# Turning two more block pairs on VectorE, all of them loaded by SyncE, with later stores and smaller warm-up matmuls, in a matmul with rotary embedding

## The chip, the cores and the metric

The kernel runs on one NeuronCore of one Trainium2 chip. The metric is device time in microseconds (us), the median of the runs shown; a change is given as a difference from it.

## The reference

```python
batch, seq, hidden, n_heads = (16, 512, 768, 12)
...
y = np.matmul(x, weight)                       # (16, 512, 768) x (768, 768)
y = y.reshape(batch, seq, n_heads, head_dim)   # head_dim 64
y1, y2 = y[..., :32], y[..., 32:]
out1 = y1 * cos1 - y2 * sin1                   # cos, sin: (seq, 64), one row for each position
out2 = y2 * cos2 + y1 * sin2
out = np.concatenate([out1, out2], axis=-1)    # float32, shape of x
```

All inputs and the output are float32. x and the output have 25.17 MB each.

## The kernel before, in words

**Tiles and groups.** The 8192 rows of x are worked in 64 tiles of 128 rows (`NTILE`), four tiles to a group (`QB`), sixteen groups (`NG`, the last is `LAST` = 15). A tile holds every fourth position of one batch entry (`where`). Two neighbouring tiles of a group are a pair: pair (g, 0) holds tiles 4g and 4g+1, pair (g, 1) the other two.

**From x to the matmul.** TensorE needs x with the hidden dimension on the partitions, in fp16. There are two ways to it, and the dictionary `BLOCKS` says which pair goes which way.

- An ordinary tile is loaded by one DMA of SyncE (SP) into one of `NX` buffers xs (`load`), cast to fp16 by ScalarE (ACT; `castx`, xc), turned by twelve small TensorE (PE) matmuls against an identity (`turn_rows`, L275), and copied from PSUM to an xt buffer by ACT.
- A block pair is loaded in four quarters (`load_quarter`, L229) whose rows are laid out such that VectorE (DVE) alone can finish the turn with one 32x32 block transpose (`turn_pair`, L303). A pair marked "sp" is loaded by SP in float32 into one of `NB` buffers xb, and ACT casts it to xd (`cast_pair`). A pair marked "pool" is loaded by GpSimd's (POOL's) queue, which casts in the DMA, into one of `NBH` buffers xh; ACT has nothing to do for it. PE does nothing for a block pair.

Before the change there are fourteen block pairs, twelve "sp" and two "pool", (4, 1) and (6, 1).

**Order of SP's loads.** The list `fetch` is written ahead. A pair that stands in `EARLY` has its quarters in its tiles' place in the list; the quarters of the others, here (5, 1), (7, 1) and (15, 1), are spread behind ordinary tiles from one to two groups ahead. `pump` takes from the list as far as buffers are free, and the semaphores hold SP until ACT has read the buffer's old content.

**Matmul.** Each tile's 768 columns are made in six steps of the hidden dimension (`CHUNKS`). PE runs two streams, one for each half of its rows, over six PSUM banks that hold one group's 3072 columns (`walk`, `both`, L365). The first group and the last tiles go by L340. The turning of tiles is written into PE's order three tiles ahead (`T_AHEAD`), ACT's casts five (`C_AHEAD`), DVE's block transposes four (`B_AHEAD`).

**Rotary part.** A group is cut into units of 512 or 1024 columns (`units`). For each, DVE multiplies PSUM by cos and sin in one instruction (`rope`, L446) into one of three homes of 3072 numbers, two in tq and one in the weights' raw buffer; POOL adds the products into an output buffer ov (L468). There are four ov buffers, one for each group in turn, so group g writes where group g-4 stood, and its adds wait for the stores of that group.

**Stores.** Groups 0 to 12 are stored in quarters by ACT's queue (`store_half`): quarter n of this sequence (four for each group) is issued at the end of tile i, with i from a formula (L678), after a wait for PE to have come so far. Groups 13 and 14 are stored by SP in halves, and group 15 by SP and ACT in pieces.

**Start.** While the first loads come, PE multiplies zeros (`warm`, L582): nine matmuls ahead of the first tile's turn and three behind it. Each has 128 weight columns and 512 moving columns, and matmul k writes bank k mod 6. The last six also leave the banks at zero for the first group, which adds onto them.

Of the kernel before, what the change touches and what calls it, by code (L numbers as in the profile page):

```python
# [16 lines left out]
class Flow:  # L17
# [24 lines left out]
    def do(self, e, make, reads=(), writes=(), dma=None, tick=True, after=0):  # L42
        need = {}
        for k in reads:
            for s, v in self.wrote.get(k, {}).items():
                need[s] = max(need.get(s, 0), v)
        for k in writes:
            for d in (self.wrote, self.readby):
                for s, v in d.get(k, {}).items():
                    need[s] = max(need.get(s, 0), v)  # L50
        if e == "pe":
            need.pop("pe", None)
            if after:
                need["pe"] = after
        waits = self.settle(e, need)
        for s, v in waits[:-1]:
            self.eng[e].wait_ge(self.sem(s), v)  # L57
        i = make(self.eng[e])
        if waits:
            s, v = waits[-1]  # L60
            i.wait_op(self.sem(s), v, "sem-ge")
        name, step = (dma, 16) if dma else (e, 1)
        self.sem(name)
        self.order[name] = len(self.order) + sum(self.count.values())
        at = self.count[name] + step
        if tick or dma:
            i.then_inc(self.sems[name], step)
            self.count[name] = at
            self.known[name, at] = dict(self.seen[e])
        for k in reads:  # L70
            d = self.readby.setdefault(k, {})
            d[name] = max(d.get(name, 0), at)
        for k in writes:
            self.wrote[k] = {name: at}
            self.readby[k] = {}
        return i
# [32 lines left out]
def kernel(  # L109
# [11 lines left out]
    f = Flow(nc, tc)  # L121
    do = f.do
    P = nc.NUM_PARTITIONS
# [9 lines left out]
    QB = 4  # L133
# [3 lines left out]
    LAST = NG - 1  # L137


    BLOCKS = {}  # L140
    for g in range(5, 14):
        BLOCKS[g, 1] = "pool" if g % 2 == 0 and g >= 4 else "sp"
    BLOCKS[LAST, 1] = "sp"
    BLOCKS[4, 1] = "pool"
    EARLY = ((3, 1), (8, 0), (8, 1), (9, 1), (10, 0), (10, 1), (11, 1), (12, 1), (13, 1))
    for p in EARLY:
        BLOCKS[p] = "sp"

    def sbuf(name, shape, dt):
        return nc.alloc_sbuf_tensor(name, shape, dt).ap()  # L150

    NX, NB, NBH, NC, NCP, NXT, NXP, NOV = 10, 3, 3, 5, 2, 8, 4, 4

    ident = sbuf("ident", [P, P], FP16)
    cold = sbuf("cold", [P, 512], FP16)
# [26 lines left out]
    py = nc.alloc_psum_tensor("py", [P, 6 * 512], FP32).ap()  # L182
# [14 lines left out]
    def where(i):  # L197
        g, s = divmod(i, QB)
        return QB * (g // SB) + s, g % SB

    def pair_of(i):
        return i // QB, (i % QB) // 2

    def is_block(i):
        return pair_of(i) in BLOCKS

# [11 lines left out]
    def load_quarter(gh, q):  # L218
        g, h = gh
        b, r = where(g * QB + 2 * h)  # L220
        e = BLOCKS[gh]
        src = x[b : b + 2].rearrange("b (j a r) (q k) -> r q a (b j) k", r=SB, a=R, q=NQ)
# [282 lines left out]
    def store_half(g, h, c, at):  # L505
# [20 lines left out]
       reads=["ident"], writes=["ident32"])  # L526
# [13 lines left out]
    fetch, quarters = [], []  # L540
    soon = [p for p in sorted(BLOCKS) if BLOCKS[p] == "sp" and p not in EARLY]
    for i in range(QB, NTILE):
# [3 lines left out]
        if not is_block(i):  # L546
            fetch.append(i)
            for _ in range(2 if i == QB * (LAST - 1) else 1):
                if quarters:
                    fetch.append(quarters.pop(0))  # L550
        elif pair_of(i) in EARLY:
            fetch += [(pair_of(i), q) for q in ((0, 2), (1, 3))[i % 2]]
# [23 lines left out]
    WARM = 12  # L576
    warmed = [0]

    def warm(k):
        for _ in range(k):  # L580
            b = warmed[0] % 6
            do("pe", lambda eng: eng.matmul(  # L582
                py[:, ts(b, 512)], cold[:, 0:P], cold, start=True, stop=warmed[0] < WARM - 6),
                reads=["cold"], writes=[f"ps{b}"], tick=False)
            warmed[0] += 1

    def mm0(i, c):
# [10 lines left out]

    U0 = units(0)
    warm(9)  # L600
    castx(0, "act")
    turn(0, "dve")
    castx(1, "act")
    warm(3)
    turn(1, "dve")
    castx(2, "act")
# [13 lines left out]
    for c in CHUNKS[3:5]:  # L620
# [8 lines left out]
        reads=["sin", "csn1", "cos"], writes=["csn"])  # L629
# [45 lines left out]
    stores, halves = {}, {}  # L675
    for n in range(4 * (LAST - 2)):
        g, (h, c) = n // 4, divmod(n % 4, 2)
        i = 5 + n + min(3, n // 5) if g < LAST - 4 else QB * (LAST - 2) + (n - 4 * (LAST - 4)) // 2  # L678
        halves.setdefault(i, []).append((g, 2 * h, c))
    for g in range(LAST - 2, LAST):  # L680
        for h in (0, 2):
# [22 lines left out]
    for i in range(QB, NTILE):  # L704
        g, s = divmod(i, QB)
# [16 lines left out]
        for n, p in enumerate(pieces(g, s)) if i >= ROWS else ():  # L722
# [3 lines left out]
            for c in CHUNKS:  # L726
                mm_piece(i, p, c, c == CHUNKS[0], c == CHUNKS[-1],
                         tick=c == CHUNKS[-1])
# [60 lines left out]
```

## Time and profile before

| what | value |
|---|---|
| median of 3 runs (lowest, highest) | 150.32 us (149.86, 150.71) |
| the profiled execution: its own time, its span | 148.68 us, 146.9 us |
| busy: PE, DVE, POOL, ACT | 140.0, 128.0, 116.7, 76.5 us |
| one turn of a tile: twelve L275 matmuls | 190 ns each in the record, overlapped; 11.6 us busy for 360 |
| ACT: cast of a tile, copy of a turned tile, cast of a pair | 910, 801, 1632 ns |
| DVE: block transpose from xd, from xh | 966 ns x12, 1246 ns x2 |
| DVE: product of 512, of 1024 columns | 1213 to 1220, 2266 to 2268 ns |
| POOL: add of 512, of 1536 columns; issue of one cast load | 1274, 3468 ns; 601 ns x8 |
| DMA | 52.44 MB, mean 357 GB/s |

The profiled execution took 1.8 us more than its span, and 1.64 us less than the median of the runs. PE is busy nearly all the time, but so are DVE and the DMA engines over most of the span; which of them sets the end has to be read stage by stage. The granted clock is shown as 1.00 throughout.

### The profile page before, as it was taken

Reading aid. Unit: us, or ns where it says so; the run is one execution under the profiler, and the core shown is the slowest. Engines: PE = TensorE matmul, PEld = TensorE weight load, DVE = VectorE, ACT = ScalarE, POOL = GpSimd, SP = SyncE. Lnnn points to the kernel's source line nnn. Section 1 sums busy time; section 2 is a strip of 40 time slices with the busy share of each in tenths; the row PEclk is TensorE's granted clock in tenths of the full one; section 3 lists DMA queues with packets and bytes.
Section 4 is the critical chain, followed back from the end, with each engine's and each line's share of the span. In section 5 each row is a group of like instructions: output and inputs, shape, how many; then the busy total and the mean of one; then the engine's idle time right before and its main releaser. Section 6 shows DMA issues by size and latency. Waiting matters only on the chain.

```text
span 146.9 us, 4261 instructions
## 1 busy us (share of the span) xinstructions
PE 140.0 (95%) x1846; PEld 112.1 (76%) x1846; DVE 128.0 (87%) x105; ACT 76.5 (52%) x84; POOL 116.7 (79%) x64
## 2 busy tenths in 40 slices
PE   6969999999999999999999999999999999999980
PEld 2445578888888888888888888888888888765860
DVE  0155999878989999899999999999989899999990
ACT  3453798788242933557442942284664649931010
POOL 2000399999996988959788988989899999899980
PEclk9999999999999999999999999999999999999999
DMA  4999999999999999999999999999999999999684
GB/s 118 379 403 404 402 401 270 263 332 327 329 332 330 339 390 389 383 345 375 377 386 384 389 395 387 396 392 393 385 388 398 392 404 401 394 412 360 267 314 158
DMA packets 37826, 52.44 MB, mean 357 GB/s; under 512 B 4656, under 2 KB 31024, under 8 KB 37808
## 3 DMA queue, kind: packets, MB, share of 16 engines
q1 hardware_dynamic: 21200, 30.42, 59.2%
q10 hardware_dynamic: 14432, 20.97, 38.6%
q0 software_dynamic: 2176, 0.79, 4.3%
q8 instruction: 14, 0.23, 0.6%
q14 instruction: 4, 0.03, 0.1%
HBM read 27.79 MB, written 25.17 MB: 361 GB/s over the span
## 4 chain that ended last, share of the span: by engine, by line
PE 83%; DVE 12%; issue 2%; DVEq 0%; SPq 0%
PE py L365 69%; DVE tq L446 8%; PE py L340 5%; PE py L582 4%; PE pt L275 3%; DVE w_raw L446 2%; PE pt L260 2%; DVE ov L415 1%; DVE py L408 0%; DVE xs L408 0%; DVE xt L194 0%; DVE w_sb L194 0%; DVE cold L519 0%; DVEq L57 0%; DVEq L784 0%
## 5 line engine op out<-in xcount | busy, mean ns | idle before, releaser
L468 POOL TENSOR_TENSOR ov<-tq 128x512 f32<-128x512 f32 (+3 forms) x34 | 76.1, 2258 | 22.4 <-DVE tq L446 21.8
L446 DVE TENSOR_TENSOR tq<-py,csn 128x1024 f32<-128x1024 f32 (+2 forms) x51 | 74.2, 1491 | 2.9 <-PE py L365 1.9
L365 PE MATMUL py<-w_sb,xt 64*128 64x512 f16 (+1 forms) x672 | 64.1, 323 | 0.0
L365 PE MATMUL py<-w_sb,xp 64*128 64x256 f16 (+1 forms) x624 | 58.7, 323 | 0.0
L365 PEld LDWEIGHTS py<-w_sb,xt 64*128 64x128 f16 x672 | 47.3, 94 | 8.8 <-DVE tq L446 0.4
L365 PEld LDWEIGHTS py<-w_sb,xp 64*128 64x128 f16 x624 | 44.2, 94 | 7.2
L194 ACT COPY xt<-pt 128x768 f16<-128x768 f16 x34 | 27.1, 801 | 33.2 <-PE pt L275 31.3
L194 ACT CAST xc<-xs 128x768 f16<-128x768 f32 x36 | 32.5, 910 | 18.3 <-PE py L365 10.5
L468 POOL TENSOR_TENSOR ov<-w_raw 128x1536 f32<-128x1536 f32 (+2 forms) x15 | 35.4, 2372 | 3.0 <-DVE w_raw L446 2.9
L446 DVE TENSOR_TENSOR w_raw<-py,csn 128x1024 f32<-128x1024 f32 (+1 forms) x22 | 35.2, 1600 | 2.5 <-PE py L365 2.1
L194 ACT CAST xd<-xb 128x1536 f16<-128x1536 f32 x12 | 19.6, 1632 | 4.0 <-PE py L365 4.0
L340 PE MATMUL py<-w_sb,xt 128*128 128x256 f16 (+1 forms) x102 | 16.8, 317 | 1.1 <-DVE w_sb L194 1.1
L340 PEld LDWEIGHTS py<-w_sb,xt 128*128 128x128 f16 x102 | 9.4, 98 | 6.7 <-DVE w_sb L194 2.0
L275 PEld LDWEIGHTS pt<-ident,xc 64*128 64x128 f16 x360 | 11.6, 95 | 1.2 <-issue 0.2
L275 PE MATMUL pt<-ident,xc 64*128 64x64 f16 x360 | 11.6, 190 | 0.0
L303 DVE STREAM_TRANSPOSE xp<-xd 128x768 f32<-128x768 f32 x12 | 11.6, 966 | 0.0
L582 PE MATMUL py<-cold 128*128 128x512 f16 x12 | 5.5, 630 | 1.4 <-DVE cold L519 1.4
L194 DVE COPY xt<-pt 128x768 f16<-128x768 f16 x2 | 1.1, 558 | 5.8 <-PE pt L260 5.8
L194 DVE CAST w_sb<-w_raw 128x768 f16<-128x768 f32 x6 | 3.3, 557 | 2.7 <-DMA w_raw<-in_weight_dram 2.6
L194 ACT COPY ov<-py 128x256 f32<-128x256 f32 x1 | 0.4, 372 | 10.0 <-PE py L478 10.0
L229 POOL DMA_DIRECT2D xh<-in_x_dram x8 | 4.8, 601 | 0.0
L582 PEld LDWEIGHTS py<-cold 128*128 128x128 f16 x12 | 1.6, 145 | 3.6 <-issue 2.2
(26 smaller groups left out, 24.5 us busy)
## 6 DMA issues: line engine op xcount, KB each, us to landing
out_dram<-ov ACTq DMA_DIRECT2D x53, 384.0 KB, 7.6
xs<-in_x_dram SPq DMA_DIRECT2D x36, 384.0 KB, 11.7
xb<-in_x_dram SPq DMA_DIRECT2D x48, 192.0 KB, 10.5
out_dram<-ov SPq DMA_DIRECT2D x4, 768.0 KB, 6.0
w_raw<-in_weight_dram SPq DMA_DIRECT2D x6, 384.0 KB, 7.0
xh<-in_x_dram POOLq DMA_DIRECT2D x8, 96.0 KB, 15.3
out_dram<-ov SPq DMA_DIRECT2D x1, 384.0 KB, 2.3
out_dram<-ov SPq DMA_DIRECT2D x3, 128.0 KB, 2.1
```

The costliest lines, as they stand in the source:

```text
L194: eng.copy(out=o, in_=i_) if e == "act" else eng.tensor_copy(out=o, in_=i_)
L229: do(e, lambda eng: eng.dma_start(out=dst[ts(q, R)], in_=src[r, q]), writes=[f"{name}q{q}"], dma=name)
L260: do("pe", lambda eng: eng.transpose(pt[:, t, h, :], src[:, t, h, :], ident), reads=[f"xc{c}", "ident"], writes=[f"pt{k}"], tick=(t, h) == ...
L275: do("pe", lambda eng: eng.transpose(pts[r][:, t, h, :], src[rows, t, h, :], ident[rows, rows]), reads=[f"xc{c}", "ident"], writes=[f"pt{r ...
L303: do("dve", lambda eng: eng.transpose(out=dst, in_=src), reads=rd, writes=[f"xp{z}"])
L340: do("pe", lambda eng: eng.matmul(ps, get(t, h), w_sb[:, t, h, a - s * H : z - s * H], start=start, stop=stop), reads=[key, f"w{t}{h}"], w ...
L365: do("pe", lambda eng: eng.matmul(py[:, a:z], get(t, h)[rows], w_sb[rows, t, h, a - s * H : z - s * H], start=start, stop=not opens and en ...
L415: do("dve", lambda eng: eng.tensor_tensor(out=ov_b[o][:, ds(c0, w)].rearrange("p (h t d) -> p h t d", t=2, d=HD), in0=q.rearrange("p (h t ...
L446: do("dve", lambda eng: eng.tensor_tensor(out=tq.rearrange("p j (h d) -> p j h d", d=D), in0=ps.rearrange("p (h d) -> p h d", d=D) .unsque ...
L468: do(adder, lambda eng: eng.tensor_tensor(out=ov_b[o][:, ds(c0, w)].rearrange("p (h t d) -> p h t d", t=2, d=HD), in0=tq[:, 0].rearrange(" ...
L582: do("pe", lambda eng: eng.matmul(py[:, ts(b, 512)], cold[:, 0:P], cold, start=True, stop=warmed[0] < WARM - 6), reads=["cold"], writes=[f ...
```

## The change

Four things are edited.

1. The block pairs become sixteen, all "sp". New are (6, 0) and (12, 0), so four more tiles are turned by DVE and not by PE; (4, 1) and (6, 1) go from POOL's queue to SP's, and ACT casts them. All pairs but (15, 1) stand in `EARLY`, so that (5, 1) and (7, 1) too have their quarters in their tiles' place. POOL issues no loads.
2. The buffers: eleven xs for ten, four xb for three, no xh for three. The memory is the same.
3. The stores on ACT's queue: quarters 25 to 33 are issued one tile later, 34 to 42 two, and 43 to 51 three (by the formula these are groups 6 to 12).
4. The first six of the twelve matmuls of zeros become eight each, with 64 weight columns and 64 moving columns: 48 in the place of six. They are still ahead of the first tile's turn, and the number of moving columns is the same.

```diff
-    BLOCKS = {}
-    for g in range(5, 14):
-        BLOCKS[g, 1] = "pool" if g % 2 == 0 and g >= 4 else "sp"
-    BLOCKS[LAST, 1] = "sp"
-    BLOCKS[4, 1] = "pool"
-    EARLY = ((3, 1), (8, 0), (8, 1), (9, 1), (10, 0), (10, 1), (11, 1), (12, 1), (13, 1))
+    BLOCKS = {(LAST, 1): "sp"}
+    EARLY = ((3, 1), (4, 1), (5, 1), (6, 0), (6, 1), (7, 1), (8, 0), (8, 1), (9, 1), (10, 0), (10, 1), (11, 1), (12, 0), (12, 1), (13, 1))
     for p in EARLY:
         BLOCKS[p] = "sp"
...
-    NX, NB, NBH, NC, NCP, NXT, NXP, NOV = 10, 3, 3, 5, 2, 8, 4, 4
+    NX, NB, NBH, NC, NCP, NXT, NXP, NOV = 11, 4, 0, 5, 2, 8, 4, 4
...
             b = warmed[0] % 6
-            do("pe", lambda eng: eng.matmul(
-                py[:, ts(b, 512)], cold[:, 0:P], cold, start=True, stop=warmed[0] < WARM - 6),
-                reads=["cold"], writes=[f"ps{b}"], tick=False)
+            n = 64 if warmed[0] < WARM - 6 else 512
+            for c in range(0, 512, n):
+                do("pe", lambda eng: eng.matmul(
+                    py[0:min(P, n), ds(b * 512 + c, n)], cold[:, 0:min(P, n)], cold[:, ds(c, n)],
+                    start=True, stop=warmed[0] < WARM - 6),
+                    reads=["cold"], writes=[f"ps{b}"], tick=False)
...
-        i = 5 + n + min(3, n // 5) if g < LAST - 4 else QB * (LAST - 2) + (n - 4 * (LAST - 4)) // 2
+        i = 5 + n + min(3, n // 5) + max(0, (n - 16) // 9) if g < LAST - 4 else QB * (LAST - 2) + 3 + (n - 4 * (LAST - 4)) // 2
```

## The prediction

> **What bounds the kernel now.** I read the page first: busy shares, slices, DMA.
>
> ```profile
> PE 140.0 (95%) x1846; PEld 112.1 (76%) x1846; DVE 128.0 (87%) x105; ACT 76.5 (52%) x84; POOL 116.7 (79%) x64
> ...
> DMA  4999999999999999999999999999999999999684
> GB/s 118 379 403 404 402 401 270 263 332 327 329 332 330 339 390 389 383 345 375 377 386 384 389 395 387 396 392 393 385 388 398 392 404 401 394 412 360 267 314 158
> ...
> q0 software_dynamic: 2176, 0.79, 4.3%
> ```
>
> PE, DVE and DMA all look full, so shares decide nothing. The chain of waits, in order of time (start, duration), does:
>
> ```profile
> 55.73 0.17 PE pt L275 x10
> 55.91 1.92 PE py L365 x19
> 57.83 0.20 PE pt L275 x11
> 58.03 5.85 PE py L365 x54
> ...
> 124.55 3.44 DVE tq L446 x3
> ...
> 142.91 0.42 DVE ov L415
> ```
>
> From 8.8 to 124.5 us it is PE with no gap: a group with one block pair takes 0.17 + 1.92 + 0.20 + 5.85 = 8.14 us. From 124.55 it is DVE to the end. The timeline of DVE shows how closely it follows (start, duration, in brackets the idle time before):
>
> ```profile
> 59.25 1.23 DVE L446 TENSOR_TENSOR w_raw<-py,csn 128x1024 f32<-128x1024 f32 x1 [0.54 <-PE py L365]
> ...
> 67.40 1.23 DVE L446 TENSOR_TENSOR tq<-py,csn 128x1024 f32<-128x1024 f32 x1 [0.27 <-POOL ov L468]
> ...
> 107.45 1.23 DVE L446 TENSOR_TENSOR w_raw<-py,csn 128x1024 f32<-128x1024 f32 x1 [0.46 <-PE py L365]
> ...
> 115.60 2.36 DVE L446 TENSOR_TENSOR tq<-py,csn 128x1024 f32<-128x1024 f32 x2 [0.53 <-PE py L365]
> ```
>
> These are the third units (second half) of groups 5, 6, 11 and 12. Between 67.4 and 107 us DVE lists no wait, and after 115.60 none before the end stage. So DVE has under 1 us of slack late in the kernel, and a gain on PE only counts if DVE can follow.
>
> **Turning on DVE.** PE loses four tiles' turns (tiles 24, 25, 48, 49). Two cost 0.17 + 0.20 = 0.37 us in the chain, so PE is 0.37 us earlier from tile 26 on and 0.74 from tile 50 on. DVE gains two block transposes. From start to next start one costs 0.89 us (68.54 to 69.43), one from xh 1.17 (60.39 to 61.56); two of the latter become the former. DVE: 2 x 0.89 - 2 x 0.28 = +1.22 us. The ledger, at the third unit of each group:
>
> - group 5: PE delivers at 59.25 - 0.37 = 58.88; DVE was free at 59.25 - 0.54 = 58.71 and has 0.89 more, 59.60. Late by 0.35 against before.
> - group 6: DVE was free at 67.13; + 0.35 - 0.28 = 67.20; PE 67.03. Now 0.20 early.
> - groups 7 to 10: DVE is dense in both kernels; 0.20 early stays.
> - group 11: DVE was free at 106.99; - 0.20 + 0.89 = 107.68, where PE would deliver at 107.45 - 0.74 = 106.71. Late by 0.23.
> - group 12: DVE was free at 115.07; + 0.23 = 115.30; PE 114.86. Early by 0.30.
> - behind it DVE is dense to the end: -0.3 us.
>
> Bounds: -0.74 if DVE overlapped its transposes with waits that the listing doesn't show, +1.22 if none of its idle time could be used. The listed waits (0.54, 0.46, 0.53) are where the ledger uses them, so I take -0.3; reading starts in place of ends (records overlap by up to 0.1) it is -0.5. I use -0.4. PE does not stall on DVE: the largest lag, 107.68 - 106.71 = 0.97 us, compares with 124.55 - (115.60 + 8.15) = 0.80 in group 13 before, which PE rode out.
>
> ACT: four pair casts more (6.5 us), four casts and four copies fewer (4 x 1.711 = 6.8): nothing, at 52% busy. POOL: eight issues fewer, 4.8 us at 24 to 33 us, where it lagged; it waits for DVE afterwards anyway: nothing.
>
> **Loads.** POOL's two pairs held 16 engines for 4.3% of 146.9 = 6.3 us. As 768-byte packets on SP's queue (36 ns each in the packet records) they take 2048 x 36 / 16 = 4.6 us. Two pairs from whole rows (512 packets of 3072 bytes at 122 ns, 3.9 us) to quarters (4.6) cost 0.7. Besides, all traffic ran at 322 GB/s in 26.25 to 50.70 us, with these loads in flight, against 390 in 75 to 99: 24.45 x 68 / 390 = 4.3 us of transfer time. So 3 to 5 us of DMA work go. [...] In the profiled execution the relief is worth nothing on the path: after the start one load alone was late,
>
> ```profile
> ACT xc L194 <- DMA xs<-in_x_dram: 1.5, 1, 1.5
> ```
>
> (waits of 100 to 147 us), five tiles ahead of use, and PE did not notice. SP's queue takes eight more quarters at some 0.5 us, under 9 us of issue in 120. A pair needs four free xb; the fifth before it is cast at least eight tiles (16 us) ahead: covered. If that cover were gone, PE would stand for the landing time, 10.5 us less the lead.
>
> **Stores.** Nobody waits for a store but POOL's adds, four groups later, and the end. Quarters of group 11 now go out near 124 to 127 us; at 7.6 us to landing (the page) they are in by 134.6 at the latest, and group 15's adds begin at 137.0. Group 10's last, near 122.4, is in at 130; its second half is overwritten from 133.3. Covered by 2.4 us or more. On ACT's queue, behind the moved stores stand only copies of tiles that PE needs three tiles later.
>
> The end is closer. In the tail the windows show (PE, PEld, DVE, ACT, POOL busy; clock, DMA share, GB/s):
>
> ```profile
> 123.00:131.00 8.00, 8.00 (x117) 5.68 (x113) 7.96 (x8) 6.04 (x8) 7.35 (x7) 1.00 1.06 401
> 131.00:139.00 8.00, 8.00 (x73) 5.83 (x71) 7.83 (x10) 0.80 (x1) 8.00 (x7) 1.00 0.83 323
> 139.00:147.00 8.00, 3.51 (x29) 2.81 (x26) 4.30 (x10) 0.37 (x1) 3.69 (x4) 1.00 0.65 242
> ```
>
> After the change eight quarters (3.15 MB), SP's four halves (3.15) and group 15 (1.57), 7.87 MB, remain at 124.1 us. At 401 GB/s they end at 143.7, at 386 at 144.5; the last piece was issued at 143.4 and its packets ended near 145.2. So the tail just fits: 0, up to +1.0 if the rate falls to 370 (145.4) and the last pieces queue. I take 0.
>
> **Matmuls of zeros.** Six of 512 columns take 6 x 0.427 = 2.56 us (weight loads start at 2.24, 2.67, 3.09). Nearest rows for the small ones: the first turn's six of 128 columns take 0.64 us, 107 ns each; half the width gives 53 ns, 48 x 53 = 2.56: no change. If the cost did not shrink with width, 48 x 107 = 5.1, +2.6 us. Below: at the pace of L275 (16 ns, at twice the clock) 1.5 us, but tile 0's cast ends at 5.1 and its turn starts at 5.2, so a gain is excluded. Behind them wait both first turns, DVE's copies and the first weight cast; PE's first matmul at 8.78 starts the gapless chain, so a delay goes to the end nearly whole. I take 0.
>
> Sum: -0.4 + 0 + 0: 148.3 us for the profiled execution, and on the median, 1.64 us above it, 149.9.
>
> **Rivals.**
> B, faster: the ordinary runs are 1.64 us longer than the profiled one. If that is loads that come late there (DMA is full from 3 to 133 us, and one load was 1.5 us late even here), the 3 to 5 us of relief and the later stores, which leave loads the engines, remove 1 to 1.6 of it: 149.9 less 1.0 = 148.9. Against it: in the profile PE never waits for a load.
> C, tail: the later stores queue before group 15's: +0.9 on A, 150.8. For it: the 7.87 MB above. It decides below about 380 GB/s.
> D, slower: the clock. The warm matmuls run at 427 ns for 512 columns; later 4608 columns take 1.95 us (217 ns). It doubles somewhere between 7.0 and 9.9 us. If the small ones do not count as activity, the rise comes their length, 2.56 us, later; half of that is lost once PE is dense, +1.3 us, and 48 x 107 would add more: 151.2 alone, up to 152.5 with that. It decides when the rise falls behind 8.8 us. Against it: zeros at full array width raised the clock. [...]
> That the change does not do what it says is excluded: the built order has 348 turning matmuls for 396.
>
> **Numbers.** A (149.9; 149.2 to 150.6 by the ledger's and tail's bounds) 0.42; B (148.2 to 149.3) 0.28; C (150.5 to 151.2) 0.15; D (151 to 152.5) 0.15. A measurement tells about 0.5%, 0.75 us, from no change: below 149.57 lie B and a quarter of A, 0.38; above 151.07 most of D and half of C, 0.21; between 0.41. The range leaves out D's upper half and B's lowest part: 148.2 to 151.5.
>
> **What would show it.** Right: 312 turns of 64 columns for 360, less missing records; third unit of group 11 waiting on nothing; DVE's last chain starting near 124.2; no q0; slices 7 to 13 near 390 GB/s; SP's last packets before 145. Wrong: L582 ending after 5.5 us or the first L340 after 9 (D); DMA full to the end and ACT's or SP's last stores landing over 3 us after issue (C); PE waiting for DVE in group 11 or 12.

## The result, and the profile after

| | before | after |
|---|---|---|
| median (lowest, highest) | 150.09 us (148.86, 150.71) | 154.46 us (153.88, 155.1) |
| ratio, 95% interval | | 1.0335 (1.0286 to 1.0384) |
| profiled execution: own time, span | 148.68, 146.9 us | 155.1, 153.3 us |

The change makes the kernel slower by 4 to 6 us. The profiled execution of after is 6.4 us longer than that of before, in span and in own time; that is 2 us more than the medians differ, since it sets one of before's shortest executions beside after's longest. Ratios, here and below, leave out executions over 1.5% above the fastest of their kernel (four of the twelve of e9, at 151.3 to 154.1 us, one or two in some other kernels), while medians have them in. Lines of the code stand four lower in after (L446 is L442, L365 is L361, L303 is L299, L194 is L190, L229 is L225).

The page of after, the rows that answer to those shown of before (shares, slices of 3.83 us, queues):

```profile
PE 141.9 (93%) x1840; PEld 115.4 (75%) x1840; DVE 129.1 (84%) x107; ACT 76.8 (50%) x80; POOL 112.3 (73%) x56
...
PEclk9999999999999999999999999999999998699999
DMA  4999999999999999999999999999999998999993
GB/s 135 317 398 401 400 402 245 271 379 397 320 366 384 300 313 392 363 375 354 387 387 373 290 347 390 384 342 359 303 280 402 396 404 328 374 381 371 391 353 131
...
q1 hardware_dynamic: 24976, 31.99, 63.4%
...
L271 PE MATMUL pt<-ident,xc 64*128 64x64 f16 x312 | 11.0, 192 | 2.3 <-ACT xt L190 2.3
```

What the change was to do to PE it did: 312 turning matmuls, q0 is gone. But the DMA engines are now full, but for one 8, to the second last slice, where before they fell to 6, 8 and 4 tenths; the rate has dips to 280 to 303 in the second half; and the clock has a dip near 130 us that before doesn't have. The waits say what was late (total, times, longest):

```profile
ACT xd L190 <- DMA xb<-in_x_dram: 16.9, 9, 3.8
ACT xc L190 <- DMA xs<-in_x_dram: 14.6, 8, 3.9
```

All the waits for xb and 5.7 us (four waits) of those for xs come after 20 us; before, ACT had one late load there, of 1.5 us. The chain that ended last, which before was PE from 8.8 us on, now goes through a load (start, duration):

```profile
112.65 13.62 DMA xb<-in_x_dram
126.29 1.57 ACT xd L190
127.85 0.70 ACT xt L190
128.96 3.34 PE py L361 x18
132.63 1.22 PE py L361 x10
133.94 0.81 DVE tq L442
```

The last quarter of pair (15, 1) is issued at 112.65 us and is in 13.6 us later; ACT casts the pair, and behind it the copy of a turned tile, for which PE stood. The timeline of DVE in after shows the same place (idle time before in brackets):

```profile
61.53 1.21 DVE L442 TENSOR_TENSOR w_raw<-py,csn 128x1024 f32<-128x1024 f32 x1
...
109.46 1.21 DVE L442 TENSOR_TENSOR w_raw<-py,csn 128x1024 f32<-128x1024 f32 x1
...
127.89 0.98 DVE L299 STREAM_TRANSPOSE xp<-xd 128x768 f32<-128x768 f32 x1 [2.33 <-ACT xd L190]
128.79 3.45 DVE L442 TENSOR_TENSOR tq<-py,csn 128x1024 f32<-128x1024 f32 x3
133.94 3.49 DVE L442 TENSOR_TENSOR tq<-py,csn 128x1024 f32<-128x1024 f32 x3 [1.71 <-PE py L361]
```

Against before, read at the same steps of DVE:

| step of DVE | before | after | after minus before |
|---|---|---|---|
| second unit of group 1 | 26.30 | 28.34 | +2.04 |
| third unit of group 5 | 59.25 | 61.53 | +2.28 |
| third unit of group 6 | 67.40 | 69.09 | +1.69 |
| third unit of group 10 | 99.38 | 101.08 | +1.70 |
| third unit of group 11 | 107.45 | 109.46 | +2.01 |
| third unit of group 12 | 115.60 | 117.48 | +1.88 |
| start of the last chain | 124.55 | 128.79 | +4.24 |
| end of DVE's last add (L415) | 143.33 | 149.24 | +5.91 |
| end of the span | 146.9 | 153.3 | +6.4 |

So 2.0 us are lost before 27 us, nothing in the nine groups behind it, 2.4 between group 12 and the last chain (the late load), 1.7 behind it (PE, which stood from 126.3 to 128.6 for a turned tile and then ran at half clock, 129.3 to 132.8 in the granted clock's record), and 0.5 in the last stores.

### The profile page after: what moved, and what is told of

Read it like the earlier page. It is cut to its first block, busy times and chain, and to the rows that moved or that the text cites. A ratio compares the mean times of both kernels' runs of the same rounds, so it can differ in the third digit from the quotient of the medians.

```text
span 153.3 us, 4249 instructions
## 1 busy us (share of the span) xinstructions
PE 141.9 (93%) x1840; PEld 115.4 (75%) x1840; DVE 129.1 (84%) x107; ACT 76.8 (50%) x80; POOL 112.3 (73%) x56
## 2 busy tenths in 40 slices
DMA packets 39426, 53.23 MB, mean 347 GB/s; under 512 B 2672, under 2 KB 33136, under 8 KB 39408
## 3 DMA queue, kind: packets, MB, share of 16 engines
HBM read 27.79 MB, written 25.17 MB: 345 GB/s over the span
## 4 chain that ended last, share of the span: by engine, by line
PE 41%; DMA 24%; SPq 16%; DVE 8%; ACT 3%; issue 3%; ACTq 1%; DVEq 0%
PE py L361 37%; DMA xb<-in_x_dram 18%; SPq L225 8%; DMA xs<-in_x_dram 6%; SPq L210 5%; DVE tq L442 4%; PE pt L271 2%; DVE w_raw L442 2%; SPq L232 2%; ACT xd L190 1%; ACT xc L190 1%; ACTq L510 1%; ACT xt L190 1%; PE py L336 1%; PE pt L256 1%
## 5 line engine op out<-in xcount | busy, mean ns | idle before, releaser
L442 DVE TENSOR_TENSOR tq<-py,csn 128x1024 f32<-128x1024 f32 (+2 forms) x51 | 74.3, 1491 | 4.3 <-PE py L361 4.0
L361 PE MATMUL py<-w_sb,xp 64*128 64x256 f16 (+1 forms) x720 | 65.5, 323 | 0.0
L361 PEld LDWEIGHTS py<-w_sb,xp 64*128 64x128 f16 x720 | 51.8, 94 | 7.4 <-DVE w_raw L442 0.2
L361 PE MATMUL py<-w_sb,xt 64*128 64x512 f16 (+1 forms) x576 | 56.4, 329 | 0.0
L361 PEld LDWEIGHTS py<-w_sb,xt 64*128 64x128 f16 x576 | 41.8, 95 | 8.2 <-issue 1.4
L190 ACT CAST xc<-xs 128x768 f16<-128x768 f32 x32 | 28.8, 905 | 21.8 <-DMA xs<-in_x_dram 14.6
L442 DVE TENSOR_TENSOR w_raw<-py,csn 128x1024 f32<-128x1024 f32 (+1 forms) x22 | 35.2, 1599 | 2.7 <-PE py L361 2.3
L190 ACT COPY xt<-pt 128x768 f16<-128x768 f16 x30 | 23.9, 800 | 22.5 <-PE pt L271 21.2
L190 ACT CAST xd<-xb 128x1536 f16<-128x1536 f32 x16 | 26.0, 1625 | 17.0 <-DMA xb<-in_x_dram 16.9
L336 PE MATMUL py<-w_sb,xt 128*128 128x256 f16 (+1 forms) x102 | 17.0, 317 | 1.4 <-DVE w_sb L190 1.1
L299 DVE STREAM_TRANSPOSE xp<-xd 128x768 f32<-128x768 f32 x16 | 15.4, 965 | 2.7 <-ACT xd L190 2.7
L336 PEld LDWEIGHTS py<-w_sb,xt 128*128 128x128 f16 x102 | 9.2, 98 | 7.4 <-DVE w_sb L190 2.7
L580 PE MATMUL py<-cold 128*64 128x64 f16 (+1 forms) x54 | 5.2, 275 | 1.4 <-DVE cold L515 1.4
L190 DVE CAST w_sb<-w_raw 128x768 f16<-128x768 f32 x6 | 3.3, 558 | 3.5 <-DMA w_raw<-in_weight_dram 3.5
L190 DVE COPY xt<-pt 128x768 f16<-128x768 f16 x2 | 1.1, 558 | 5.5 <-PE pt L256 5.5
L190 ACT COPY ov<-py 128x256 f32<-128x256 f32 x1 | 0.4, 372 | 10.0 <-PE py L474 10.0
L580 PEld LDWEIGHTS py<-cold 128*64 128x64 f16 (+1 forms) x54 | 3.3, 154 | 2.0 <-DVE cold L515 1.4
```

The costliest lines, as they stand in the source:

```text
L190: eng.copy(out=o, in_=i_) if e == "act" else eng.tensor_copy(out=o, in_=i_)
L299: do("dve", lambda eng: eng.transpose(out=dst, in_=src), reads=rd, writes=[f"xp{z}"])
L336: do("pe", lambda eng: eng.matmul(ps, get(t, h), w_sb[:, t, h, a - s * H : z - s * H], start=start, stop=stop), reads=[key, f"w{t}{h}"], w ...
L361: do("pe", lambda eng: eng.matmul(py[:, a:z], get(t, h)[rows], w_sb[rows, t, h, a - s * H : z - s * H], start=start, stop=not opens and en ...
L442: do("dve", lambda eng: eng.tensor_tensor(out=tq.rearrange("p j (h d) -> p j h d", d=D), in0=ps.rearrange("p (h d) -> p h d", d=D) .unsque ...
L580: do("pe", lambda eng: eng.matmul(py[0:min(P, n), ds(b * 512 + c, n)], cold[:, 0:min(P, n)], cold[:, ds(c, n)], start=True, stop=warmed[0] ...
```

## The experiments

All times are compared with runs of the kernel before on the same chip (149.10 to 149.43 us). "Ratio" is to those.

### One part at a time

The change has three parts that can be taken singly: the loads (pairs, their order, buffers), the stores, the matmuls of zeros. Five kernels undo one or do one alone:

**e1: after, with the old store times.**

```diff
-        i = 5 + n + min(3, n // 5) + max(0, (n - 16) // 9) if g < LAST - 4 else QB * (LAST - 2) + 3 + (n - 4 * (LAST - 4)) // 2
+        i = 5 + n + min(3, n // 5) if g < LAST - 4 else QB * (LAST - 2) + (n - 4 * (LAST - 4)) // 2
```

> The changed kernel with the stores at their old tiles; the 16 pairs and the small matmuls of zeros stay. Theory S (the later stores empty the store queue, and loads alone, with quarters among them, move at some 250 GB/s in place of 390, so that loads come late): about 4 us of the 4.4 lost come back, but not the 2 us of the start: 152 us or a little less, and no second with load packets alone after 35 us. Theory L (sixteen pairs of 768-byte packets, in their tiles' place, are themselves too slow): no change, 154.4 us, and the late casts of pairs stay.

Measured: 151.94 us, ratio 1.0151 (1.0079 to 1.0223). Taking the later stores out of after gives 2.7 us back by the ratios. Theory S has the time right, but not for its reason: the loads are as late as in after (by the measure of the table under e12 and e13, 119.7 us for 119.1), and microseconds with load packets alone remain at 40, 51 and 52 us.

**e2: after, with the old matmuls of zeros** (six of 512 columns for the 48 small ones).

```diff
-            n = 64 if warmed[0] < WARM - 6 else 512
-            for c in range(0, 512, n):
-                ...
+            do("pe", lambda eng: eng.matmul(
+                py[:, ts(b, 512)], cold[:, 0:P], cold, start=True, stop=warmed[0] < WARM - 6),
+                reads=["cold"], writes=[f"ps{b}"], tick=False)
```

> The changed kernel with the old twelve matmuls of zeros. Theory W (the 96 further PE instructions move the first 16 KB instruction fetch from 22.4 us to 14.5 us, into the way of tile 4's load): the fetch goes back to about 22 us, tile 4 is cast near 15.5 us and not 17.4, and the whole kernel gains up to 2 us: 152.5 us. Theory N (the late start is chance of that run): 154.4 us.

Measured: 153.21 us, ratio 1.0258 (1.0197 to 1.0319): 1.25 us back, between the two theories. The instruction packet is back at 22.8 us and tile 4 is cast at 15.80 us, as theory W has it; the second unit of group 1 starts at 26.70, where before has 26.30 and after 28.34. (The small matmuls are 84 instructions more, 42 matmuls and 42 weight loads, and not 96.)

**e3: before, with only the later stores** (the edit of e1 the other way round).

> The kernel before with the later stores alone. Theory S: loads come late as in the changed kernel, 2 to 4 us slower, 152 to 154 us. Theory L: the stores cost nothing by themselves, 150.1 us.

Measured: 151.42 us, ratio 1.0142 (1.0072 to 1.0212). Neither theory has it: the loads aren't late (26 MB of them started at 115.6 us, 115.4 in before) and VectorE is hardly later than before (last chain 125.15, last add's end 143.92 for 143.33), so the loss lies behind it. The windows of e3 and the page's windows of before in the prediction have the same form (PE, PEld, DVE, ACT, POOL busy; clock, DMA share, GB/s):

```profile
123.00:131.00 8.00, 8.00 (x127) 5.80 (x120) 7.92 (x9) 6.61 (x8) 7.39 (x7) 1.00 0.89 330
131.00:139.00 8.00, 8.00 (x70) 5.72 (x69) 7.83 (x9) 0.80 (x1) 8.00 (x8) 1.00 1.04 376
139.00:147.00 8.00, 4.11 (x34) 3.34 (x32) 4.89 (x11) 0.37 (x1) 4.25 (x4) 1.00 1.02 382
```

From 139 to 147 us the DMA engines are full at 382 GB/s, where before they stood at a share of 0.65. From 123 to 131 us it is the other way round, 0.89 and 330 GB/s for 1.06 and 401: nearly all loads are in (all but 0.03 MB by 124 us), and the moved stores aren't issued yet. By the packet records the last store's packets end at 148.1 us, for 145.2 before.

**e4: before, with only the 48 small matmuls of zeros** (the edit of e2 the other way round).

> The kernel before with the 48 small matmuls of zeros alone. Theory W: the first instruction fetch at 14 to 15 us, tile 4's cast 1 to 2 us later, 151.5 to 152 us. Theory N: 150.1 us.

Measured: 150.63 us, ratio 1.0081 (1.0046 to 1.0116). The timelines of PE and ACT in e4:

```profile
1.41 4.16 PE L584 MATMUL py<-cold 128*64 128x64 f16 x51 [1.41 <-DVE cold L519]
```

```profile
16.95 1.88 ACT L194 CAST xc<-xs 128x768 f16<-128x768 f32 x2 [3.34 <-DMA xs<-in_x_dram]
```

The small matmuls take no longer than the large ones (before: to 5.43 us, here to 5.57), and PE's first real matmul is at 8.00 us, earlier than before's 8.78. What is late is a load: tile 4's cast starts at 16.95 for 15.41 before, after a wait of 3.34 us for 2.35. Half of this is SP's issue of the load, at 7.50 us for 6.75; from the issue to the cast it is 9.45 us for 8.66. The cost is less than the 1.4 to 1.9 us of theory W. The page has one packet queue that bears on it, q8, "instruction", with packets of 16 KB: its first one lies at 14.8 us here and at 22.4 us before.

**e5: only the loads part** (after with the old stores and the old matmuls of zeros: sixteen pairs, all by SP, eleven xs, four xb).

> The changed kernel with the old store times and the old matmuls of zeros: the sixteen pairs, their order and their buffers alone. If the three parts add (small matmuls +1.5 us, later stores +2.3 us against before), about 1 us is left of the 4.9 lost here: 150.2 us. My ledger of the prediction for this part: 0.4 us faster than before, 148.7 us. Theory L would have it at 152 us or more.

Measured: 150.44 us, ratio 1.0094 (1.0061 to 1.0127). The parts alone add up, within their intervals: 1.0081 and 1.0142 and 1.0094 give 1.0317, where after has 1.0335. DVE's timeline in e5 shows where its part is lost:

```profile
121.14 3.84 DVE L442 TENSOR_TENSOR w_raw<-py,csn 128x1024 f32<-128x1024 f32 x3
126.55 0.98 DVE L299 STREAM_TRANSPOSE xp<-xd 128x768 f32<-128x768 f32 x1 [1.56 <-ACT xd L190]
127.45 3.45 DVE L442 TENSOR_TENSOR tq<-py,csn 128x1024 f32<-128x1024 f32 x3
```

### The matmuls of zeros: the number of instructions, or their size

**e7: before, with 24 matmuls of 128 columns for the first six** (18 matmuls and 18 weight loads more, for e4's 42 and 42).

```diff
+            n = 128 if warmed[0] < WARM - 6 else 512
+            for c in range(0, 512, n):
+                ...
```

> The kernel before with the first six matmuls of zeros as four each of 128 columns: 24 for 6, so 36 PE instructions more and not 84, the same number of columns. Theory W (the place of the instruction fetch): the fetch comes between 15 and 22 us, behind tile 4's load, whose cast stays near 15.5 us, and the cost is under 0.5 us: 149.1 to 149.6 us. Theory N2 (many narrow matmuls as such cost the time, by the clock or by their issue): a part of the 1.5 us in proportion, 0.6 us or more.

Measured: 149.65 us, ratio 1.0024 (0.9994 to 1.0054). The instruction packet lies at 17.7 us, and tile 4's cast starts at 15.33, as before. Over all kernels run here the two go together: with the packet at 14.5 to 15.2 us (the five with the small matmuls) tile 4 is cast at 16.95 to 17.52; with it at 17.7 us or later (the fifteen others) at 15.2 to 16.3. SP issues that load anywhere from 6.7 to 8.1 us in both sets; from its issue to the cast it is 9.45 to 10.09 us in the five and 8.06 to 8.82 in the others, 1.2 us more on the mean. So what goes with the cost is the number of instructions, and the early place of the instruction packet, not PE's time. That the packet itself holds tile 4's load back for this 1.2 us is the likeliest reading, but was not tested apart from the instructions.

### The loads: which pairs, and why

**e6: the loads part, with all stores two tiles earlier.** It leaves the very first store quarter out, and some later pieces may be stored ahead of their last adds.

```diff
-        i = 5 + n + min(3, n // 5) if g < LAST - 4 else QB * (LAST - 2) + (n - 4 * (LAST - 4)) // 2
+        i = 3 + n + min(3, n // 5) if g < LAST - 4 else QB * (LAST - 2) - 2 + (n - 4 * (LAST - 4)) // 2
```

> The same with all of ACT's stores two tiles earlier than before the change. Theory S (an empty store queue leaves loads alone at 250 GB/s): the store queue is never empty after 30 us, loads are in time, and this is 1 us or more faster than the same with the old store times. The rival (stores take engine time from loads, so earlier stores make loads later): it is slower by 0.5 us or more.

Measured: 154.23 us, ratio 1.0306 (1.0259 to 1.0353), 3.8 us over e5. Earlier stores are no help, but neither theory says why: the loads are no later than in e5 (26 MB started at 118.1 us for 118.7, the last quarter of (15, 1) in at 124.22 us for 124.89). ACT is. It issues its stores in order with its casts; of the two shown here the first waited for POOL's adds until 124.37 us, and the second was issued by 125.79:

```profile
122.79 3.00 ACTq L510 DMA_DIRECT2D out_dram<-ov  x2
125.83 1.54 ACT L190 CAST xd<-xb 128x1536 f16<-128x1536 f32 x1 [2.13 <-POOL ov L464]
```

The cast of (15, 1) starts 1.6 us after its load is in; VectorE waits 3.25 us for it, PE 2.80 us for the copy behind it, and the clock then falls for 3.4 us. So e6 shows what it costs when ACT comes to a store before POOL's adds are done, and doesn't settle what stores do to loads.

**e8: after, with a pair's quarters fetched in the order 0, 1, 2, 3** in place of 0, 2, 1, 3.

```diff
-            fetch += [(pair_of(i), q) for q in ((0, 2), (1, 3))[i % 2]]
+            fetch += [(pair_of(i), q) for q in ((0, 1), (2, 3))[i % 2]]
```

> The changed kernel with the quarters of a pair in the order 0, 1, 2, 3 in place of 0, 2, 1, 3. [...]

Measured: 154.71 us, ratio 1.0384 (1.0351 to 1.0417); the interval meets that of after. By the ratios the order costs 0.7 us, which the intervals don't tell from nothing. In the trace loads are slower than in after (325 GB/s from 95 to 121 us for 350), the last quarter of (15, 1) is in at 127.70 us for 126.26, and the slowest microsecond of loads alone moves 160 GB/s for 235 in after (behind 30 us). It is one execution, the longest of the four, so whether the order of the quarters slows the loads stays open.

**e9: e5 without the two new pairs** (fourteen pairs, all by SP in their tiles' place).

```diff
-    EARLY = ((3, 1), (4, 1), (5, 1), (6, 0), (6, 1), (7, 1), (8, 0), ..., (11, 1), (12, 0), (12, 1), (13, 1))
+    EARLY = ((3, 1), (4, 1), (5, 1), (6, 1), (7, 1), (8, 0), ..., (11, 1), (12, 1), (13, 1))
```

> The loads part without its two new pairs: (4, 1), (5, 1), (6, 1), (7, 1) by SP in their tiles' place, eleven xs and four xb, but (6, 0) and (12, 0) stay ordinary; stores and matmuls of zeros as before. Theory T (the two new pairs cost the loads part its 1.2 us: at groups 11 to 13 VectorE has more turns while their loads come late): this kernel is at the time of before or a little under it, ratio 0.995 to 1.002, with VectorE's last product chain starting at 124.0 to 124.8. Theory Q (the quarters that moved from GpSimd's queue and from behind ordinary tiles into their place cost it: they sit in SP's queue ahead of whole rows that are needed): ratio 1.006 to 1.010, with late loads of xb again.

Measured: 150.25 us, ratio of the compared runs 1.0018 (0.998 to 1.0056).

**e10: before with only the two new pairs added.**

```diff
-    EARLY = ((3, 1), (8, 0), (8, 1), (9, 1), (10, 0), (10, 1), (11, 1), (12, 1), (13, 1))
+    EARLY = ((3, 1), (6, 0), (8, 0), (8, 1), (9, 1), (10, 0), (10, 1), (11, 1), (12, 0), (12, 1), (13, 1))
```

> The kernel before with only (6, 0) and (12, 0) added as SP pairs in their tiles' place; (4, 1) and (6, 1) stay on GpSimd's queue, (5, 1) and (7, 1) spread, buffers as before. By the prediction's ledger VectorE gains two block transposes, +1.78, less the idle time it can use in groups 5, 6, 11 and 12: about +0.2 us at the end without lateness of loads, ratio 1.000 to 1.003. Theory T: ratio 1.006 to 1.012, and the waits for xb or xs in groups 10 to 13 grow. Theory Q: ratio 0.999 to 1.004.

Measured: 150.86 us, ratio 1.0107 (1.006 to 1.0154). Its chain of waits goes through the same load as after's:

```profile
112.11 12.28 DMA xb<-in_x_dram
124.42 1.60 ACT xd L194
```

**e11: before with only (5, 1) and (7, 1) in their tiles' place.**

```diff
-    EARLY = ((3, 1), (8, 0), ...
+    EARLY = ((3, 1), (5, 1), (7, 1), (8, 0), ...
```

> The kernel before with (5, 1) and (7, 1) in their tiles' place and nothing else changed. Theory Q: part of the 1.2 us, ratio 1.002 to 1.006. Theory T: no change, 0.998 to 1.002.

Measured: 149.31 us, ratio 0.9984 (0.9954 to 1.0014). So theory T stands and Q falls: the two new pairs alone cost all that the loads part costs. This rests on e10 and e11; the executions of e9 spread too far, from 148.81 to 154.12 us, to carry it.

**e12 and e13: the same stores left out of before and of e5.** Each leaves one store quarter of groups 5 to 10 unwritten, 2.36 MB of the output.

```diff
+        if 5 <= g <= 10 and n % 4 == 3:
+            continue
         halves.setdefault(i, []).append((g, 2 * h, c))
```

> The kernel before without one store quarter in each of groups 5 to 10 (that sixteenth of the output, in all 2.36 MB of 25.17, isn't written): some 6 us of DMA time go, at 391 GB/s. It is the yardstick of the next run. Both theories: little gain, since PE and VectorE set its pace when loads are in time: 148.6 to 149.4, ratio 0.995 to 1.000.

> The loads part alone (sixteen pairs, stores and matmuls of zeros as before), also without these six store quarters (2.36 MB of the output aren't written). Theory F (the DMA engines were full: a quarter's bytes cost 36.2 / 768 = 47 ns for each 1000 bytes against 39.7 in whole rows, and the two new pairs' loads came late): with 6 us of DMA time given back its cost goes, and the prediction's ledger holds: -0.6 to +0.4 us against the run e12, with few waits for xb or xs after 95 us. Theory G (VectorE can't take two more turns, whatever the loads do): it stays 1.0 to 1.6 us over e12, as with all stores (1.0094).

Measured: e12 148.78 us, ratio 0.9966 (0.9944 to 0.9987); e13 148.67 us, ratio 0.9962 (0.9931 to 0.9993). With 2.36 MB less to move the loads part costs nothing: theory F, the DMA engines' time, stands, and G falls: the last quarter of (15, 1) is in at 122.10 us, 124.89 in e5. (The edit also takes six issues off ACT's queue, which these runs don't separate.) One detail of F's expectation was missed: waits for xb remain in e13,

```profile
ACT xd L190 <- DMA xb<-in_x_dram: 14.6, 7, 3.6
```

but the last block transpose waits 0.93 us for its cast, not 1.56 as in e5, and the last chain starts at 124.65 us, as in before.

The packet records give the measure behind this, the time at which 26 of the 27.53 MB of x and weights were started (the tables of cos and sin not counted, the pairs of POOL's queue by what is read):

| | before | e9 | e10 | e5 | after | e12 | e13 |
|---|---|---|---|---|---|---|---|
| 26 MB loaded at, us | 115.4 | 116.6 | 118.1 | 118.7 | 119.1 | 112.3 | 115.9 |
| DVE's last chain starts at, us | 124.55 | 125.50 | 126.94 | 127.45 | 128.79 | 124.73 | 124.65 |

Where the loads are late, the last chain is late by about as much (in after the 2.0 us of the head are part of it). Loads that come early, as in e12, bring it no earlier than in before: there PE and DVE set it.

**e15, e16, e17: pair (15, 1) cast and turned two tiles later**, in before, in e5 and in after. In e5 and after the last late load is that of this pair, which PE needs only in group 15; ACT and VectorE take it in order during group 13.

```diff
-        if i == QB * (LAST - 2) + 2:
+        if i == QB * (LAST - 2) + 4:
             cast_pair((LAST, 1))
...
-        bturns(i + (B_AHEAD if i < QB * (LAST - 2) else 9))
+        bturns(i + (B_AHEAD if i < QB * (LAST - 2) else 7))
```

> The kernel before with pair (15, 1) cast and turned two tiles (about 4 us) later. Both theories: its load is in time in the kernel before, so little changes: ratio 0.996 to 1.003.

> The loads part alone (sixteen pairs, stores and matmuls of zeros as before), with pair (15, 1) cast and turned two tiles (about 4 us) later. Theory I (ACT and VectorE stand in order behind a load that is needed only in group 15; in the loads part ACT cast it at 124.91 us, VectorE waited 1.56 us for it, PE 1.11 us for the copy behind it): most of the part's 1.4 us goes, ratio 0.998 to 1.004, with the last chain starting at 125.0 to 126.0 us. Theory J (the ordinary tiles' own loads are late, 1.9 us at 120.84, and PE starves whatever stands between): ratio 1.007 to 1.012.

> The kernel after with the same edit. Theory I: 1.5 to 3 us under after, since PE's stall of 2.3 us at 126.3 us and the half clock behind it go too: ratio 1.014 to 1.024. Theory J: as after, 1.029 to 1.038.

Measured: e15 150.58 us, ratio 1.012 (1.0067 to 1.0173); e16 153.02 us, 1.0247 (1.0196 to 1.0298); e17 154.59 us, 1.0361 (1.0324 to 1.0398). e17 lies in the range of theory J; e16 lies above both ranges, and e15, which was to change little, lost 1.8 us. The timeline of DVE in e15, where the load was in time (at 122.36 us):

```profile
123.94 3.49 DVE L446 TENSOR_TENSOR tq<-py,csn 128x1024 f32<-128x1024 f32 x3
128.87 0.98 DVE L303 STREAM_TRANSPOSE xp<-xd 128x768 f32<-128x768 f32 x1 [1.44 <-ACT xd L194]
```

The cast was put so late in ACT's order that it starts at 127.23 us, after VectorE has come to the turn. VectorE again waits, now for the order of ACT and not for the load. So these runs don't tell I from J; they show that this cast has no room for two tiles' delay. In before it ends at 123.63 us, and the turn starts at 123.65.

**e18: e5, with only VectorE's turn of (15, 1) moved back**, behind three more products; ACT's order is as in e5.

> The loads part alone (sixteen pairs, stores and matmuls of zeros as before), with VectorE's turn of pair (15, 1) three products later, and ACT's cast of it left where it was. If the loads part lost its time at VectorE's 1.56 us of waiting for that cast: ratio 0.998 to 1.004, the three products from about 125.9 us. If the delay reaches VectorE by another way too (PE's 1.11 us of waiting for the copy behind the cast): ratio 1.004 to 1.012, VectorE waiting for PE behind the turn in place of ACT ahead of it.

Measured: 151.21 us, ratio 1.0106 (1.006 to 1.0153), as e5 or a little over. The profiled execution is one of the kernel's longest (153.02 us), and only the order of its waits is read: VectorE no longer waits for ACT at the turn, but for PE ahead of the products around it (0.41, 0.50 and 0.73 us), and PE waits 1.26 us for the tile copy that stands behind the cast of (15, 1). So in this execution the late load reaches the end by two ways, through VectorE's own order and through ACT's and PE's, and closing one opens the other.

**e14: before, with ACT's stores in whole rows** (one DMA of 3072-byte rows at the second quarter's place, for two of 1536).

```diff
-        W = H // 2
+        W = H
...
-        halves.setdefault(i, []).append((g, 2 * h, c))
+        if c == 1:
+            halves.setdefault(i, []).append((g, 2 * h, c))
```

> The kernel before with ACT's stores in whole rows: at the second quarter of each half one DMA of 3072-byte rows takes the place of two of 1536. In the trace of before a store packet of 1536 bytes took 65.5 ns (95 to 121 us) and a load packet of 3072 bytes 122 ns, so 19.66 MB of stores would take some 3.5 us less of the 16 engines, if rows stored cost what rows loaded cost. Theory F: where loads were a little late in the ordinary runs they come in time: 0 to -1.0 us, ratio 0.993 to 1.000. Rival: the first quarter of each half goes out one tile (2 us) later, and the tail piles up as in e3: +0.5 to +1.0 us, ratio 1.003 to 1.007.

Measured: 154.49 us, ratio 1.0303 (1.025 to 1.0357): wrong by both theories. The store packets did become cheaper, 124.7 ns for 3072 bytes (105 to 120 us) where two of 1536 took 131.2. But the load packets beside them became dearer: from 95 to 121 us one of 768 bytes took 41.6 ns for 36.2, one of 3072 bytes 147.7 for 122. 26 MB were loaded at 117.8 us, PE stood again for 3.14 us up to 128.4 us, and the clock fell for 3.4 us. The edit also issues the first quarter of each half later, so that size and time of the stores changed together. No version that beats the kernel before was found.

## Why the prediction was wrong

The sign was wrong: "same" was the likeliest case, "slower" had 0.21, and the range ended at 151.5 us. The sum was -0.4 for the turning and nothing for the rest; what it put at nothing measured +1.4 us (the loads part, e5), +2.1 (stores, e3) and +1.2 (matmuls of zeros, e4). Point by point:

**Turning on DVE: right, to 0.3 us.** Less the 2.04 us of the head, after's third units stand at +0.24, -0.35, -0.34, -0.03 and -0.16 us in groups 5, 6, 10, 11 and 12; the ledger had +0.35, -0.20, -0.20, +0.23, -0.30. PE didn't wait for DVE there. The gain of 0.3 to 0.5 at the end is not seen: e13, where the loads cost nothing, is 0.11 us under e12, within the spread of both.

**Loads: the step whose mechanism failed.** "Worth nothing on the path" and "covered" rested on a cast at least 16 us ahead of the buffer's next use, and on 10.5 us from issue to landing. In after that load took 13.6 us, and SP issued it late, behind loads that themselves waited for the full engines. The prediction counted some 0.5 us for the issue of a quarter; here twelve took 16.85 us, with no wait for a semaphore in the trace from 80 to 114 us, so SP's queue had no spare time:

```profile
83.31 16.85 SPq L225 DMA_DIRECT2D xb<-in_x_dram  x12
```

A pair takes one xb, too, not four, so that the buffer it waits for is that of the fourth pair before it. The cover was counted in buffers, but the supply was bytes: from 95 to 121 us the engines were full in both kernels, and before moved 393 GB/s there, e10 369, after 350. What was asked of them grew on three sides at once. The pairs' quarters need more engine time than whole rows (the prediction's 0.7 us); PE, 0.74 us faster, wants its tiles that much earlier; and the mix itself ran slower, with 768-byte packets at 39.6 ns in e10 for 36.2 in before, and 3072-byte ones at 131 for 122. How much each of the three adds was not measured. The price of the part is +1.4 us (e5, 0.9 to 1.9 by its interval), where the sum had zero, and -0.4 for the turning.

**The relief of 3 to 5 us was a misreading.** The slices show 322 GB/s while POOL's casting loads were in flight, and the prediction took the gap to 390 as lost time. But the page counts these loads by the bytes they write: q0 has 0.79 MB for two pairs that are 1.57 MB in HBM, and the totals of the two pages differ by just that, 52.44 and 53.23 MB, at the same "HBM read 27.79 MB". Counted by what is read, the 322 GB/s are 353, and after, without any casting load, has 351 in the same window, so the rest of the gap to 390 isn't theirs. From 30 to 52 us before moved 367 GB/s, e9 365 and after 360. With that, rival B loses the relief that it rested on, and e9, in which the two pairs did move to SP, shows no gain (1.0018).

**Stores: right mechanism, wrong size.** Rival C had the tail pile up at +0.9 us, the sum at zero; e3 measured +2.1, with VectorE only 0.6 us later. Three things were off. The bytes left at 124 us were 7.87 MB by the prediction; by the packet records e3 had 8.51, nearly all of them stores, and after 9.93, of which 0.46 were loads. The rate in the tail was 376 to 382 GB/s, not 386 to 401, about the 380 below which C was to decide: 8.51 MB at 379 is 22.5 us, to 146.5. And the engines weren't full up to there: by the packet records e3 moved 287 GB/s at a share of 0.78 from 122 to 127 us, where before had 395 at 1.06, for loads were ending and the moved stores not yet issued. The last piece ended at 148.1. In after, the stores cost 2.7 us (e1). How that divides between the tail and what is lost ahead of it was not measured: e1's last chain starts at 127.36 us, after's at 128.79, and e1 has no fall of the clock.

**Matmuls of zeros: the price was right, its place wasn't looked for.** 48 small matmuls took as long as six large ones, 4.16 us for the 51 that the profile groups, as estimated (53 ns each). Rival D's clock did not come late: the granted clock rose at 6.45 us in after, 7.17 in before, 4.6 to 7.4 in the profiles of all kernels, and the last three matmuls of zeros, of 512 columns each, took 1.04 us from 6.00 in after for 1.46 from 5.86 in before. The cost, +1.2 us (e4), came with the number of instructions and not with their time on PE, most likely by way of the code that has to be fetched (e7). The prediction costed PE and left the "instruction" queue out of the account, though the page lists it.

**The signs named in advance** told the truth for C: the DMA engines are full to the end, the last stores land late, and SP's last packets end at 151.7, not before 145. Of D's two signs one was just met, the 51 grouped L580 ending at 5.56 us for 5.5, and one was not, the first L336 starting at 8.49 for 9; the clock's rise, earlier than in before, decides against D. Of the signs of being right, the 312 turns, no q0 and group 11's third unit waiting on nothing came; the last chain near 124.2 (128.79) and slices 7 to 13 near 390 (271 to 397) didn't.

## What to carry to other kernels

Where the DMA engines show 9 in every slice, a step that makes a compute engine faster asks for data earlier and so can have a price in bytes (the loads part cost 1.4 us here, e5, and nothing with 2.36 MB less to move, e13): draw up the load queue's progress (bytes started by a given time) next to the ledger of the engines, and take no buffer count for a cover. In the tail, sum all that is left, late loads too, at the rate measured there (376 to 382 GB/s in e3), before any store is moved back, and see that the engines have work between the last load and the first moved store (in e3 their share was 0.78 from 122 to 127 us). And count instructions as well as their time: 84 small ones cost 1.2 us here without making their engine any slower.

## What the runs showed of the hardware

- The cost of a packet is not its own affair. From 95 to 121 us the DMA share is 1.05 to 1.07 in all kernels, but a load packet of 768 bytes took 36.2 ns (before) to 45.1 ns (e8) there, and one of 3072 bytes 122 to 160 ns, as the loads and stores beside them were changed. In single microseconds with almost no store packets the loads of mixed quarters and rows moved only 203 to 262 GB/s (before, from 23 to 28 us), where whole rows alone had moved 396 to 412 just before (15 to 22 us) and the mix with stores beside it 393 (95 to 121 us). So in these traces it is quarters without stores beside them that are slow. Between 30 and 120 us before has no such microsecond, after has seven (235 to 276 GB/s) and e14 ten (243 to 316). That would explain why stores made fewer and larger (e14) cost 4.5 us: they leave gaps without stores. It was not tested by itself, and the reason for the low rate is open.
- In four kernels a stall of PE cost more than its length. PE stood for 2.33 us up to 128.6 us in after, and the granted clock was half for one stretch of 3.4 us behind it (129.33 to 132.75). The 17 matmuls that took 1.68 us there in before then took 3.09. The same fall stands in e2, e6 and e14, behind stalls of 2.27, 2.80 and 3.14 us; stalls of 1.98 us (e16), 2.38 us (e8) and 2.43 us (e18) had none. What sets the four apart is where the stall lies. In all twenty kernels the granted clock changed only at whole multiples of 3.413 us after its rise (the 41st in before's record; the 36th, 37th and 43rd in after's); these four falls came 122.88 us after it, at the 36th. Counted in windows of that length, PE stood for 2.08 to 3.09 us of the window before each of the four, but for at most 1.24, 1.83 and 1.58 us of any one window around the stalls of e16, e8 and e18, which lie across a window's end. Over all windows of the twenty kernels from the rise on, their ends included, the shortest standing time with a fall behind it was 2.06 us (e9), and the longest without one 2.00 us (e2).
